# The context's norms: squares and the convolution's mean added up on GpSimd, one chunk summed on TensorE

## The chip, the cores and the metric

The kernel runs on one core of one Trainium2 chip. The metric is device time in microseconds of one execution, the median of several runs. All times below are microseconds (us) unless marked ns; the engines are TensorE (PE in the rows, PEld for its weight loads), VectorE (DVE), ScalarE (ACT), GpSimd (POOL) and SyncE (SP).

## What is computed

A first block works on 256 tokens of width 1024: an adaptive norm, two kinds of attention, and a mixture of 32 experts of which each token takes four. A second block of two layers follows, which has a second stream beside the tokens, 256 tokens of context (`ctx`). In its first layer the context goes through the whole layer; in the second it gives only keys and values. Cut to what matters here, the context's way through the first layer is:

```
hc  = modulate(rms_norm_2(xc, mix_pre_g), shc1, scc1)            # norm 1
pc  = hc @ w_in                                                  # q, k, v, gates, convolution input
y   = conv_general_dilated(gl, conv_w, ...) + conv_b             # 31 taps, each channel by itself
y   = silu(layer_norm(y, conv_norm_g, conv_norm_b))              # mean, then variance
yc  = (ga * a_out + gg * g_out + gc * c_out) @ w_out
xc  = xc + gc1 * rms_norm_2(yc, mix_post_g)                      # first residual
hc2 = modulate(rms_norm_2(xc, ffn_pre_g), shc2, scc2)            # the norm ahead of the FFN
xc  = xc + gc2 * rms_norm_2(sq_relu_mlp(hc2, w_ff1, w_ff2), ffn_post_g)   # last residual
```

`rms_norm_2(x, g)` is `x * rsqrt(mean(x * x) + 1e-6) * g` over the 1024 channels of a token; `layer_norm` takes the mean away first. There are five such sums of squares over the channels on the context's way (norm 1, the convolution's norm, first residual, the norm ahead of the FFN, last residual) and one plain mean (the convolution's). The context does not depend on the first block's tokens, so its layer can run at any time before the second block needs its keys and values.

## The kernel before

**Layout.** Channels lie on the 128 partitions, in `KC` = 8 chunks, and the 256 tokens `T` along the free axis: a tile of the stream is 128x8x256. A sum over the channels is therefore a sum over the chunks and over the partitions. TensorE does it: a chunk's 128 tokens are the stationary operand, a column of ones the moving one, and the result, one value for each of 128 tokens, adds up in PSUM over the chunks (`stats_add`, L194 to L203). One such sum over eight chunks and two halves of the tokens is 16 matmuls, and since an fp32 matmul leaves two records in the trace, 32 records of 128x1.

**A norm.** `norm_sums` (L245) takes the squares of two chunks at a time into a tile of 128x512, alternately on ScalarE (L252) and VectorE (L254), and sums each with `stats_add` (L200). `stats_end` (L216) computes the reciprocal root on VectorE with small operations of 128x2 (L163 to L173) and spreads it over the partitions with two transposes (`bcast_tok`, L179), on which the elementwise work of the norm waits. `folded_stats` (L261) is another form, which the last stage of the kernel uses: ScalarE squares the first four chunks in one operation, ScalarE and VectorE the next two pairs, GpSimd adds those onto the first four (L272) and halves the four chunks to two and to one (`fold`, L187, L192), and TensorE sums that one chunk. Where `self.side` is set, the tile of the squares is `sqs`, of which there is one buffer.

**Stages.** The first block runs in three stages, `front` (the attention), `route` (the choice of the experts) and `moe` (the 32 experts). The context's layer, `ctx_pass` (L1426), is laid between them as other work for the same engines: `prio` (L1760) calls `run_ctx` (L1786) after each step of a stage, as many times as the lists FRONT, ROUTE and MOE say (L1843 to L1845), and `run_ctx` sets `self.side` while it writes a piece of the context. A scheduler then orders the instructions of each engine when the program is built; at run time every engine takes its own in that order and waits where an operand is not there. The context's pieces have PSUM buffers of their own (`side`) and pools of their own (`cx`). `conv_norm` (L1617) is called by the context (L1539) and by the last stage (L1356). Two other callers of `norm_stats`, at L517 and L709, belong to the first block and run without `self.side`. The context's layer ends with a DMA of its result (L1575); the experts go on without it, and after them the two layers of the second block run on the tokens, with `self.tail` set.

**An expert.** The tokens of an expert stand in 32 or 64 columns (`hG`). Its gate and up weights (`raw`, L981) come by DMA, are the moving operand, and fill `mlin`; a bias is added by matmuls with `bgh` and `bgl` (L1036); VectorE and ScalarE compute the activation (`eg`, L920 to L925); TensorE transposes it (L987) and multiplies the down weights (L1006) into `main`; L897 and L898 put the result back to its tokens. The context's large products are L365 (`side`).

Of the kernel before, what the change touches and what calls it, by code (L numbers as in the profile page):

```python
# [15 lines left out]
OP = mybir.AluOpType  # L16
# [4 lines left out]
P = 128  # L21
D = 1024
KC = 8
GW = 128
T = 256
# [73 lines left out]
class Builder:  # L99
# [156 lines left out]
        return st  # L256

    def norm_stats(self, xT):
        return self.stats_end(self.norm_sums(xT), 1.0 / D)

    def folded_stats(self, xT, b):  # L261
# [1355 lines left out]
    def conv_norm(self, L, yc, chi, clo, pool):  # L1617
        nc = self.nc
        self.pop_conv(1000)
        if self.tail:  # L1620
            b = self.t(pool, [P, KC, T], tag="qn")[:, 0:4, :]
            nc.gpsimd.tensor_add(b, yc[:, 0:4, :], yc[:, 4:8, :])
            self.fold(b)
            mb = self.ps("tr")[:, :T]
            nc.tensor.matmul(mb, self.ones, b[:, 0, :], start=True, stop=True)
            for c in range(0, KC, 2):
                nc.vector.scalar_tensor_tensor(yc[:, c:c + 2, :], mb.unsqueeze(1).to_broadcast([P, 2, T]), -1.0 / D,
                                               yc[:, c:c + 2, :], op0=OP.mult, op1=OP.add)
            bc = self.folded_stats(yc, self.t(pool, [P, KC, T], tag="qn")[:, 0:4, :])
        else:  # L1630
            s = self.ps("tr")
            for c in range(KC):
                for t in range(2):
                    nc.tensor.matmul(s[:, t:t + 1], yc[:, c, t * P:(t + 1) * P], self.ones[:, 0:1],
                                     start=(c == 0 and t == 0), stop=(c == KC - 1), skip_group_check=True)
            mu = self.st([P, 2], tag="mu")
            nc.vector.tensor_scalar(mu, s[:, 0:2], 1.0 / D, None, op0=OP.mult)
            mb = self.bcast_tok([mu[:, 0:1], mu[:, 1:2]])
            for c in range(KC):
                nc.vector.tensor_sub(yc[:, c, :], yc[:, c, :], mb)  # L1640
            bc = self.norm_stats(yc)
        hb = self.st([P, KC], tag="hb")
        nc.vector.tensor_scalar(hb, L["cbn"], 0.5, None, op0=OP.mult)
        for k in range(KC):
            y = self.hk()
            nc.vector.scalar_tensor_tensor(y, yc[:, k, :], L["cg"][:, k:k + 1], bc, op0=OP.mult, op1=OP.mult)
            th = self.t(pool, [P, 512], tag="cth", bufs=2)[:, :T]
            nc.scalar.activation(th, y, AF.Tanh, scale=0.5, bias=hb[:, k:k + 1])
            nc.scalar.activation(y, y, AF.Identity, bias=L["cbn"][:, k:k + 1])
            nc.vector.scalar_tensor_tensor(y, th, 1.0, y, op0=OP.add, op1=OP.mult)  # L1650
            self.split(y, chi[:, k, :], clo[:, k, :], scale=0.5)
# [234 lines left out]
```

## Time and profile before

| | us |
| --- | --- |
| median of three runs | 2740.73 (2739.36 to 2746.4) |
| the profiled execution | 2745.34 |
| its span, first to last instruction | 2743.4 |
| TensorE busy in the span | 2590.6 (94%) |
| VectorE busy | 1605.5 (59%) |
| ScalarE busy | 1177.6 (43%) |
| GpSimd busy | 318.3 (12%) |

The mean granted clock of TensorE is 0.974 of full speed. In the trace the first block's attention and routing last up to about 300 us, the experts with the context's layer beside them to about 1275 us (the context's last DMA is at 1274.46), the experts alone to about 1520 us, and the two layers of the second block from about 1595 us to the end. Busy times of one engine can be read against the stretch they stand in; TensorE's records are pipelined, so that one begins before the last has ended.

### The profile page before, as it was taken

What the parts mean: (1) busy time and instruction counts of PE and PEld (TensorE: products, weight loads), DVE (VectorE), ACT (ScalarE), POOL (GpSimd) and SP (SyncE); (2) the same over time, 40 slices, a digit from 0 to 9 for tenths busy, and PEclk for the clock granted to TensorE, in tenths of its full rate; (3) what the DMA queues carried; (4) which work ended last, traced back from release to release, by engine and by line L of the source; (5) the groups of instructions that cost most, each with busy time, mean ns of one, the idle gap of its engine ahead of it and who ended that gap; (6) DMA issues with size and microseconds to landing.
All of it is one profiled execution on the core that took longest, in us unless ns stands there. A gap on an engine that the chain in (4) does not pass through costs nothing. (4 is left out here: it accounts for less than half of the span.)

```text
span 2743.4 us, 49770 instructions
## 1 busy us (share of the span) xinstructions
PE 2590.6 (94%) x20358; PEld 2046.6 (75%) x20359; DVE 1605.5 (59%) x3058; ACT 1177.6 (43%) x2019; POOL 318.3 (12%) x334
## 2 busy tenths in 40 slices
PE   7999999999899999999889879999999999999898
PEld 5656878678677767875333468888789998899898
DVE  3465543687654524433111269988556689897655
ACT  2343343333243323331111146785444566866544
POOL 0000000000000000000000015462001034461000
PEclk9989899999999999999999989999999999999999
DMA  9758599989999999999999935335764443335352
GB/s 400 300 222 296 199 384 418 371 342 403 387 360 385 394 377 355 409 419 367 397 383 421 422 147 185 124 105 219 259 223 174 184 179 132 140 135 185 146 193 85
DMA packets 119369, 769.79 MB, mean 281 GB/s; under 512 B 11632, under 2 KB 12016, under 8 KB 52832
## 3 DMA queue, kind: packets, MB, share of 16 engines
q1 hardware_dynamic: 117744, 759.15, 70.8%
q0 software_dynamic: 1392, 7.41, 0.7%
q8 instruction: 162, 2.65, 0.4%
q14 instruction: 71, 0.58, 0.1%
HBM read 762.84 MB, written 3.67 MB: 279 GB/s over the span
## 5 line engine op out<-in xcount | busy, mean ns | idle before, releaser
L343 DVE TENSOR_TENSOR wlo<-raw,whi 128x1024 fp32r<-128x1024 f32 (+1 forms) x288 | 338.5, 1178 | 163.0 <-ACT whi L342 155.6
L365 PE MATMUL lin<-hhi,wlo 128*128 128x256 f32 x1440 | 401.3, 284 | 10.0 <-DVE wlo L343 9.6
L365 PE MATMUL lin<-hhi,whi 128*128 128x256 f32 x1440 | 399.5, 281 | 3.7 <-ACT hhi L284 2.2
L365 PE MATMUL lin<-hlo,whi 128*128 128x256 f32 x1440 | 399.1, 279 | 0.1
L342 ACT ACTIVATE whi<-raw 128x1024 fp32r<-128x1024 f32 (+1 forms) x288 | 276.9, 964 | 236.0 <-PE lin L365 164.8
L981 PE MATMUL mlin<-raw,hG 128*32 128x256 f32 (+2 forms) x2920 | 344.0, 460 | 16.2 <-DMA raw<-in_w_gate_up_dram 16.2
L365 PEld LDWEIGHTS lin<-hhi,wlo 128*128 128x128 f32 x1440 | 269.4, 189 | 24.9 <-DVE wlo L343 19.1
L1590 POOL TENSOR_TENSOR yc<-yc,ctmp 128x256 f32<-128x256 f32 x240 | 247.4, 1049 | 301.1 <-ACT ctmp L1589 300.8
L343 DVE TENSOR_TENSOR wlos<-raws,whis 128x512 fp32r<-128x512 f32 x246 | 166.3, 688 | 194.2 <-ACT whis L342 184.1
L365 PEld LDWEIGHTS lin<-hhi,whi 128*128 128x128 f32 x1440 | 271.1, 189 | 9.2 <-ACT hhi L284 3.7
L365 PEld LDWEIGHTS lin<-hlo,whi 128*128 128x128 f32 x1440 | 272.5, 189 | 2.4 <-DVE hlo L285 1.2
L981 PEld LDWEIGHTS mlin<-raw,hG 128*32 128x32 f32 (+2 forms) x2920 | 130.9, 121 | 178.8 <-issue 114.6
L342 ACT ACTIVATE whis<-raws 128x512 fp32r<-128x512 f32 x246 | 149.1, 627 | 224.8 <-PE side L365 177.5
L365 PE MATMUL side<-hhi,whis 128*128 128x256 f32 x720 | 203.2, 288 | 0.0
L365 PE MATMUL side<-hlo,whis 128*128 128x256 f32 x720 | 199.7, 282 | 0.0
L365 PE MATMUL side<-hhi,wlos 128*128 128x256 f32 x720 | 193.1, 284 | 0.7 <-DVE wlos L343 0.5
L343 DVE TENSOR_TENSOR wlo<-raws,whi 128x1024 fp32r<-128x1024 f32 x108 | 139.6, 1293 | 77.3 <-ACT whi L342 74.5
L1592 DVE SCALAR_TENSOR_TENSOR yc<-gl,cw,yc 128x256 f32<-128x256 f32 x240 | 169.4, 736 | 1.5 <-ACT yc L1586 1.5
L342 ACT ACTIVATE whi<-raws 128x1024 fp32r<-128x1024 f32 x108 | 114.5, 1060 | 129.0 <-PE lin L365 89.0
L1006 PE MATMUL main<-raw,aT 128*32 128x256 f32 (+2 forms) x1408 | 160.9, 447 | 2.3 <-DMA raw<-in_w_down_dram 2.3
L365 PEld LDWEIGHTS side<-hhi,whis 128*128 128x128 f32 x720 | 136.7, 190 | 16.4 <-issue 12.0
L365 PE MATMUL lin<-ahi,wlo 128*128 128x256 f32 x528 | 144.0, 279 | 4.7 <-DVE wlo L343 4.6
(603 smaller groups left out, 5739.3 us busy)
## 6 DMA issues: line engine op xcount, KB each, us to landing
raw<-in_w_gate_up_dram SPq DMA_DIRECT2D x120, 2048.0 KB, 11.4
raw<-in_w_down_dram SPq DMA_DIRECT2D x55, 2048.0 KB, 11.0
raw<-in_w_in_dram SPq DMA_DIRECT2D x60, 1024.0 KB, 7.1
raws<-in_w_in_dram SPq DMA_DIRECT2D x95, 512.0 KB, 6.7
raws<-in_w_ff_dram SPq DMA_DIRECT2D x88, 512.0 KB, 8.3
raw<-in_w_ff_dram SPq DMA_DIRECT2D x44, 1024.0 KB, 7.1
phi<-in_ada_w_dram SPq DMA_DIRECT2D x10, 1024.0 KB, 7.3
plo<-in_ada_w_dram SPq DMA_DIRECT2D x10, 1024.0 KB, 7.0
```

The source lines that it names most:

```text
L342: x = nc.scalar.activation(flat(hi), flat(rows[i]), AF.Copy)
L343: y = nc.vector.tensor_sub(flat(lo), flat(rows[i]), flat(hi).bitcast(F32))
L365: x = nc.tensor.matmul(*args, skip_group_check=True, **kw)
L981: nc.tensor.matmul(d, hT(k), gu[k][c0 // D][:, c0 % D:c0 % D + W], start=False, stop=(k == KC - 1), skip_group_check=True)
L1006: nc.tensor.matmul(pys[h][g * C:(g + 1) * C, :W], st, dn[m][:, c0:c0 + W], start=(m == 0), stop=(m == KC - 1), skip_group_check=True)
L1590: nc.gpsimd.tensor_add(d, d, m)
L1592: self.paced(1, nc.vector.scalar_tensor_tensor(d, x, wcol, d, op0=OP.mult, op1=OP.add))
```

## The change

Two functions are changed, and both for the context alone.

```diff
     def norm_stats(self, xT):
+        if self.side:
+            return self.folded_stats(xT, self.t(self.cx, [P, 4, T], tag="kv"))
         return self.stats_end(self.norm_sums(xT), 1.0 / D)
...
     def conv_norm(self, L, yc, chi, clo, pool):
         nc = self.nc
         self.pop_conv(1000)
-        if self.tail:
-            b = self.t(pool, [P, KC, T], tag="qn")[:, 0:4, :]
...
-        else:
-            s = self.ps("tr")
-            for c in range(KC):
-                for t in range(2):
-                    nc.tensor.matmul(s[:, t:t + 1], yc[:, c, t * P:(t + 1) * P], self.ones[:, 0:1],
-                                     start=(c == 0 and t == 0), stop=(c == KC - 1), skip_group_check=True)
-            mu = self.st([P, 2], tag="mu")
-            nc.vector.tensor_scalar(mu, s[:, 0:2], 1.0 / D, None, op0=OP.mult)
-            mb = self.bcast_tok([mu[:, 0:1], mu[:, 1:2]])
-            for c in range(KC):
-                nc.vector.tensor_sub(yc[:, c, :], yc[:, c, :], mb)
-            bc = self.norm_stats(yc)
+        four = lambda: self.t(pool, [P, KC, T], tag="qn")[:, 0:4, :] if self.tail else self.t(pool, [P, 4, T], tag="kv")
+        b = four()
+        nc.gpsimd.tensor_add(b, yc[:, 0:4, :], yc[:, 4:8, :])
+        self.fold(b)
+        mb = self.ps("tr")[:, :T]
+        nc.tensor.matmul(mb, self.ones, b[:, 0, :], start=True, stop=True)
+        for c in range(0, KC, 2):
+            nc.vector.scalar_tensor_tensor(yc[:, c:c + 2, :], mb.unsqueeze(1).to_broadcast([P, 2, T]), -1.0 / D,
+                                           yc[:, c:c + 2, :], op0=OP.mult, op1=OP.add)
+        bc = self.folded_stats(yc, four())
         hb = self.st([P, KC], tag="hb")
```

The context's norms now go through `folded_stats`, with a tile of four chunks, `kv`, from the context's pool: one square over four chunks and one over two on ScalarE, one over two on VectorE, two adds and two folds on GpSimd, then two matmuls of 128x1 (four records) instead of 16. The convolution's mean is added up by GpSimd as well and summed and spread over the partitions by one matmul of 128x256, with the matrix of ones stationary and that chunk moving; the subtraction is four operations over two chunks on VectorE instead of eight over one. The last stage of the kernel did both in this form already. In the new kernel the line numbers are two higher from `norm_stats` to `conv_norm` and ten lower behind it.

On each engine the scheduler's order moves with it. TensorE has 16815 instructions instead of 16902, VectorE 3086 instead of 3096, GpSimd 378 instead of 355.

TensorE, from the end of the context's last product ahead of the first residual to the broadcast of the norm ahead of the FFN, before. `sqs` are tiles of squares, `rs_rs` the reciprocal root, `raw` an expert's weights, `main` the accumulator of its down product:

```order
L981 MATMUL mlin_9111<-raw_9104,hG_8599 32x256 x4
L200 MATMUL side_9385<-ones_72,sqs_9398 128x1 x4
L200 MATMUL side_9385<-ones_72,sqs_9404 128x1 x4
L179 MATMUL side_9422<-cst_68,rs_rs_9412 128x128 x2
...
L200 MATMUL side_9451<-ones_72,sqs_9458 128x1 x4
...
L987 MATMUL main_9191<-cst_68,eg_9184 128x128 x2
L200 MATMUL side_9451<-ones_72,sqs_9464 128x1 x4
L1006 MATMUL main_9200<-raw_9196,aT_8890 32x256 x16
L200 MATMUL side_9451<-ones_72,sqs_9470 128x1 x4
L1006 MATMUL main_9200<-raw_1688_9198,aT_8890 32x256 x16
L179 MATMUL side_9488<-cst_68,rs_rs_9478 128x128 x2
```

The same place in the new kernel:

```order
L983 MATMUL mlin_9067<-raw_9060,hG_8555 32x256 x4
L200 MATMUL side_9351<-ones_72,kv_9341 128x1 x2
L179 MATMUL side_9366<-cst_68,rs_rs_9356 128x128 x2
...
L200 MATMUL side_9405<-ones_72,kv_9395 128x1 x2
...
L989 MATMUL main_9147<-cst_68,eg_9140 128x128 x2
L179 MATMUL side_9420<-cst_68,rs_rs_9410 128x128 x2
...
L1008 MATMUL main_9156<-raw_9152,aT_8846 32x256 x16
```

Each norm has one row of sums instead of four, and the two groups of down matmuls that stood among the sums of the second norm now stand behind its broadcast.

TensorE at the last residual, before:

```order
L365 MATMUL side_13506<-phi_12797,wlos_13620 128x256
L200 MATMUL side_13675<-ones_72,sqs_13682 128x1 x2
L1006 MATMUL main_11790<-raw_2073_11788,aT_11354 32x256 x16
L200 MATMUL side_13675<-ones_72,sqs_13688 128x1 x4
L200 MATMUL side_13675<-ones_72,sqs_13694 128x1 x4
L897 MATMUL main_11831<-G_10211,yh_11827 128x256
...
L981 MATMUL mlin_12032<-raw_12024,hG_11542 64x512 x2
...
L179 MATMUL side_13712<-cst_68,rs_rs_13702 128x128 x2
```

and in the new kernel:

```order
L367 MATMUL side_13438<-phi_12729,wlos_13552 128x256
L989 MATMUL main_11711<-cst_68,eg_11704 128x128 x4
...
L1008 MATMUL main_11722<-raw_11718,aT_11286 32x256 x16
L200 MATMUL side_13617<-ones_72,kv_13607 128x1 x2
L179 MATMUL side_13632<-cst_68,rs_rs_13622 128x128 x2
L1008 MATMUL main_11722<-raw_2068_11720,aT_11286 32x256 x16
L983 MATMUL mlin_11964<-raw_11956,hG_11474 64x512 x2
```

The broadcast follows its sums directly; the second group of down matmuls, the next expert's gate and up matmuls and the combine rows, which stood ahead of it, stand behind it.

GpSimd around the first residual, before. `pick` prepares an expert's bias row, `m_` is the load of the context's own stream:

```order
L1020 CAST pick_9100<-sel_5192 128x288
L1020 CAST pick_9246<-sel_5192 128x288
L1553 DMA m_1704_9383<-in_ctxT_dram 128x2048
L1020 CAST pick_9532<-sel_5192 128x288
L1020 CAST pick_9863<-sel_5192 128x256
```

and in the new kernel:

```order
L1555 DMA m_1701_9339<-in_ctxT_dram 128x2048
L1022 CAST pick_9464<-sel_5180 128x288
L274 TENSOR_TENSOR kv_9341<-kv_9341,sqs_9343 128x512
L274 TENSOR_TENSOR kv_9341<-kv_9341,sqs_9346 128x512
L192 TENSOR_TENSOR kv_9341<-kv_9341 128x512
L192 TENSOR_TENSOR kv_9341<-kv_9341 128x256
L274 TENSOR_TENSOR kv_9395<-kv_9395,sqs_9397 128x512
L274 TENSOR_TENSOR kv_9395<-kv_9395,sqs_9400 128x512
L192 TENSOR_TENSOR kv_9395<-kv_9395 128x512
L192 TENSOR_TENSOR kv_9395<-kv_9395 128x256
L1022 CAST pick_9795<-sel_5180 128x256
```

The eight operations of the two norms stand between two experts' `pick` rows.

## Rows read from the trace of the kernel before

**Rows 1.** Busy time by stretch: stretch, length, PE, PEld, DVE, ACT, POOL, clock, DMA share, GB/s.

```profile
300.00:1275.00 975.00, 953.93 (x8465) 719.40 (x8465) 515.30 (x1130) 343.58 (x657) 13.40 (x29) 0.98 0.94 376
1275.00:1520.00 245.00, 214.66 (x1032) 87.14 (x1030) 44.34 (x88) 28.77 (x48) 2.81 (x7) 0.97 0.99 403
```

**Rows 2.** TensorE's waits from 300 to 1275 us, the largest: sum, count, longest.

```profile
PE mlin L981 <- DMA raw<-in_w_gate_up_dram: 6.5, 4, 4.3
```

**Rows 3.** Context's sums: L200's (ns least/mean/most), TensorE groups (busy, mean ns | idle before).

```profile
L200 PE MATMUL side<-ones,sqs x160: 164/250/373, 175.3 to 1259.1; 128*128 128x1 f32 x160
...
L200 PE MATMUL side<-ones,sqs 128*128 128x1 f32 x32 | 5.7, 298 | 1.6 <-DVE sqs L254 0.8 <-ACT sqs L252 0.8
...
L1634 PE MATMUL side<-ones,y 128*128 128x1 f32 x16 | 3.6, 353 | 0.4 <-DVE y L1592 0.4
```

**Rows 4.** TensorE at the convolution's norm: start, length, instruction.

```profile
726.28 0.77 PE L1036 MATMUL mlin<-bgh,pick 128*128 128x512 f32 x1
...
737.21 0.60 PE L200 MATMUL side<-ones,sqs 128*128 128x1 f32 x4
...
751.12 3.65 PE L981 MATMUL mlin<-raw,hG 128*64 128x512 f32 x16
```

**Rows 5.** The same view from the first residual to the norm ahead of the FFN.

```profile
887.26 1.93 PE L981 MATMUL mlin<-raw,hG 128*32 128x256 f32 x32
887.88 0.63 ACT L252 ACTIVATE sqs<-y 128x512 f32<-128x512 f32 x1
...
891.01 1.09 PE L200 MATMUL side<-ones,sqs 128*128 128x1 f32 x8 [0.84 <-DVE sqs L254]
...
894.02 0.66 PE L179 MATMUL side<-cst,rs_rs 128*128 128x128 f32 x2 [1.92 <-DVE rs_rs L173]
894.61 3.64 PE L981 MATMUL mlin<-raw,hG 128*32 128x256 f32 x32
...
901.41 0.42 DVE L1734 TENSOR_TENSOR m<-m,hks 128x256 f32<-128x256 f32 x1
...
912.04 0.43 PE L179 MATMUL side<-cst,rs_rs 128*128 128x128 f32 x2
```

**Rows 6.** GpSimd's groups in the whole span, all from the last stage: busy, mean ns | idle.

```profile
L192 POOL TENSOR_TENSOR qn<-qn 128x512 f32<-128x512 f32 x4 | 8.6, 2155 | 0.3
L212 POOL TENSOR_TENSOR sq<-sq,sq 128x512 f32<-128x512 f32 x4 | 6.4, 1612 | 363.5 <-ACT sq L1395 261.3 <-ACT sq L1369 102.1
L1622 POOL TENSOR_TENSOR qn<-yc 128x1024 f32<-128x1024 f32 x2 | 6.4, 3188 | 1.8 <-DVE yc L1592 1.8
L272 POOL TENSOR_TENSOR merged<-merged,sq 128x512 f32<-128x512 f32 x2 | 3.1, 1558 | 12.9 <-ACT sq L271 12.9
L192 POOL TENSOR_TENSOR sq<-sq 128x256 f32<-128x256 f32 x4 | 3.0, 738 | 0.3
```

**Rows 7.** Squares on VectorE: context's (ns least/mean/most); last stage's with GpSimd's add beside.

```profile
L254 DVE TENSOR_TENSOR sqs<-y x6: 683/691/693, 740.3 to 1257.5; 128x512 f32<-128x512 f32 x6
...
1880.88 2.33 POOL L272 TENSOR_TENSOR qn<-qn,sq 128x512 f32<-128x512 f32 x1 [11.53 <-ACT sq L271]
...
1881.98 1.78 DVE L269 TENSOR_TENSOR sq<-yc 128x512 f32<-128x512 f32 x1
```

**Rows 8.** TensorE at the last residual, and the busy times of one stretch there.

```profile
1254.53 1.93 PE L1006 MATMUL main<-raw,aT 128*32 128x256 f32 x32
...
1260.55 5.32 PE L981 MATMUL mlin<-raw,hG 128*64 128x512 f32 x16
...
1266.84 0.38 PE L179 MATMUL side<-cst,rs_rs 128*128 128x128 f32 x2
...
1264.00:1268.00 4.00, 4.00 (x24) 1.92 (x22) 1.30 (x4) 0.00 (x0) 0.00 (x0) 1.00 0.27 53
```

**Rows 9.** TensorE behind its longest wait; busy times of one stretch, the clock third last.

```profile
718.79 3.64 PE L981 MATMUL mlin<-raw,hG 128*32 128x256 f32 x32 [4.30 <-DMA raw<-in_w_gate_up_dram]
...
720.00:724.00 4.00, 3.59 (x30) 1.94 (x22) 4.00 (x12) 0.00 (x0) 0.00 (x0) 0.50 1.00 419
```

More of the change, by code (lines that the diff above doesn't have):

```diff
@@ L1619, in conv_norm @@
         self.pop_conv(1000)
-        if self.tail:
-            b = self.t(pool, [P, KC, T], tag="qn")[:, 0:4, :]
[L1622 to L1629, printed above, removed]
-        else:
-            s = self.ps("tr")
-            for c in range(KC):
-                for t in range(2):
-                    nc.tensor.matmul(s[:, t:t + 1], yc[:, c, t * P:(t + 1) * P], self.ones[:, 0:1],
-                                     start=(c == 0 and t == 0), stop=(c == KC - 1), skip_group_check=True)
-            mu = self.st([P, 2], tag="mu")
-            nc.vector.tensor_scalar(mu, s[:, 0:2], 1.0 / D, None, op0=OP.mult)
-            mb = self.bcast_tok([mu[:, 0:1], mu[:, 1:2]])
-            for c in range(KC):
-                nc.vector.tensor_sub(yc[:, c, :], yc[:, c, :], mb)
-            bc = self.norm_stats(yc)
+        four = lambda: self.t(pool, [P, KC, T], tag="qn")[:, 0:4, :] if self.tail else self.t(pool, [P, 4, T], tag="kv")
[8 more added lines that the diff above has]
+        bc = self.folded_stats(yc, four())
         hb = self.st([P, KC], tag="hb")
```

## The prediction

> **What bounds the kernel now.** I read the busy times by stage first, then TensorE's waits, then what the replaced work costs, then its places in the order of time. The change works between the start and 1275 us. From 300 to 1275 us TensorE is busy for 953.93 of 975 us, with the DMA engines busy 0.94 of the time; VectorE works 515.30 us there and GpSimd 13.40 [rows 1]. The stage after it, MoE alone, is the transfers': DMA share 0.99, TensorE 214.66 of 245 us. So up to 1275 us TensorE's queue sets the pace as long as weights arrive, with little room in the transfers, and GpSimd is free. What TensorE waits for is short: its largest item is 6.5 us in all, for gate and up weights [rows 2]. A saved TensorE microsecond can therefore count, but so does any wait that a longer chain of GpSimd makes.
>
> **What the change removes.** Each of five context norms now sums 8 chunks by 32 matmul records of 128x1; the group is 160 records [rows 3]. Eight of them take 1.09 us [rows 5], so 160 take 160/8 x 1.09 = 21.8 us (by the front's 32 in 5.7 us [rows 3], up to 28). The convolution's mean is 16 records more, 3.6 us, with 0.4 of waiting for the last taps [rows 3]. I count another 2.2 us, an estimate: that its end at 1.2 GHz holds back the rows behind it, which begin at 726.28 [rows 4]; the two transposes of the mean are 0.6 more (such a pair takes 0.66 [rows 5]). What comes back to TensorE is 5 times four records at 0.5 us and one 128x256 matmul at 0.3 to 0.6. Net 21.8 + 3.6 + 2.2 + 0.6 - 2.5 - 0.6 = 25 us of TensorE work less. If nothing else moved, that would be the gain, 0.9%.
>
> **What it adds: a chain.** Before, the sums of early chunks ran on TensorE while the later squares were still being made, and MoE matmuls stood between them. Now one row must wait for a chain: a square on ScalarE of two chunks (0.63 us [rows 5]), a GpSimd add of 128x512, VectorE's square of the last two chunks (0.69 [rows 7]; it writes the one buffer of that name, so it waits for that add), a second add, a fold at 128x512, one at 128x256. No such GpSimd work stands in this stage before, so I bound it by the tail's: an add takes 1.56 us at the least (`merged` [rows 6]) and 2.33 beside VectorE's work [rows 7]; a fold of 512 takes 2.16 and at the least 1.61, as an add of that size does; one of 256 0.74, or by half of the 2.16 1.08 [rows 6]. VectorE's square takes 1.78 us where GpSimd's add lies beside it [rows 7]. Low end 0.63 + 1.56 + 0.69 + 1.56 + 1.61 + 0.74 = 6.8 us; high end 0.63 + 2.33 + 1.78 + 2.33 + 2.16 + 1.08 = 10.3. I take 7.8, the low end and 1 us for six hand-overs, since VectorE does little besides at these places.
>
> The Trainium skill, GPSIMD Engine Reference, sections 3.1 and 4.1, speaks against the change: an elementwise add of two inputs belongs on VectorE, where it takes about half GpSimd's time. Its figure, 4497 ns for 2048 elements, would make some 1.1 us of a 512-element add and as little of a fold, as an estimate, which the trace does not bear out: it has 1.56 to 2.33. By the page's figure the chain would be some 1.6 us shorter at four places, the sum below -3 instead of +3.3, and the time 2738.
>
> **Place by place.** TensorE takes its rows in order, so I compare how long the same rows take from one fixed point to the norm's broadcast (L179), and correct for MoE work that the new order has moved behind it.
>
> *Norm 1, in the front stage.* The 32 records there took 5.7 us with 1.6 us of waiting [rows 3]. The new chain is as long, and the front's own chain goes on through other engines: -3 us, bounds -6 and 0.
>
> *Convolution.* The mean's 3.6 + 2.2 + 0.6 = 6.4 us go. Its three GpSimd steps (3.19 + 2.16 + 1.08 = 6.4 us [rows 6]) have cover: the rows from 726.28 to 737.21, 10.9 us [rows 4], stand ahead of the new mean matmul. Without that cover they cost 6.4. From 737.21 to the broadcast, which follows the row that ends at 754.77, it was 17.5 us. Now: mean matmul 0.6, two subtractions on VectorE 1.4 (at the square's 0.69 [rows 7]), a square over four chunks 1.1 (an estimate, twice the 0.63 less its start), chain 7.8, sums 0.5, and the gate and up rows that stand ahead of the broadcast as before, 3.65 (the row at 751.12 [rows 4]): 15.0. Another 3.65 us of gate and up rows have moved behind it, so 18.6 for the same work. 18.6 - 17.5 - 6.4 = -5.3, bounds -6.3 and -2.8 by the chain's ends.
>
> *First residual.* TensorE is free for its sums at 889.2 us (887.26 + 1.93 [rows 5]). The first square begins at 887.88, so the chain ends at 895.7: TensorE stands still for 6.5 us (bounds 5.5 to 9) with its MoE rows behind that one row. Then 0.5 for the sums and 1.92 for the rsqrt: broadcast at 898.1 instead of 894.02, +4.1. From that go the sixteen records of the first four chunks, which TensorE ran before 887.26, 2 x 1.09 = 2.2 us: +1.9, bounds +0.9 and +4.4.
>
> *The norm ahead of the context's FFN.* Broadcast to broadcast it was 912.04 - 894.02 = 18.0. The last chunks are ready 7.8 us in (901.41 and 0.42 [rows 5]), the first six earlier, so ScalarE's second square comes at about 5.5. Then 5.5 + 7.8 + 0.5 + 1.92 = 15.7, and two groups of 16 down matmuls have moved behind it, 2 x 1.93 = 3.9: 19.6, so +1.6, bounds +0.6 and +4.1. VectorE's square that waits for the first add has the swiglu of the next expert queued behind it, and ScalarE and TensorE wait for that; this is the wait that the change adds on VectorE, and it lies inside the 7.8.
>
> *Last residual.* From the row at 1254.53 to the broadcast at 1266.84 it was 12.3 us, filled with one group of down rows, one of gate and up (5.32), and combine rows, of which a group fills what lies between 1265.87 and the broadcast, 1.0 [rows 8]. Now the row of sums stands behind an earlier group of down rows, so the chain begins 1.93 sooner; it is 0.6 + 7.8 + 0.5 + 1.92 = 10.8 long, and behind the broadcast 1.93 of down, 3.65 of gate and up (the undisturbed group's) and two such groups of combine rows are still to do: -1.9 + 10.8 + 7.6 = 16.5, +4.2; the two earlier pairs of records, 1.1 us, go: +3.1, bounds +2.1 and +5.6. In 1264 to 1268 us the DMA share is 0.27 [rows 8]: the transfers wait for TensorE just there, so this passes on into the transfer-bound stage.
>
> The chip's clock comes on top. After the 4.30 us wait at 718 us the gate and up group takes 3.64 us instead of 1.93, and the granted clock is 0.50 in 720 to 724 us, which is 1.2 of its 2.4 GHz [rows 9]; after the 0.84 and 1.92 us waits at the first residual the same group takes 3.64 as well, and 1.93 some microseconds before [rows 5]. Some of the old idle already costs this; the new waits make such stretches at the convolution, the FFN norm and the last residual, at 3.64 - 1.93 = 1.7 us for each group at the low clock, and some three groups' worth after a long wait. I take +5, bounds +2 and +14.
>
> Sum: -3 - 5.3 + 1.9 + 1.6 + 3.1 + 5 = +3.3; bounds -6.7 and +25 if all are low or all high together. So the waits hand back what TensorE saves. GpSimd's library load, which the order of the new kernel has near the start, is hidden, since GpSimd has nothing urgent there, and the tail's rows keep their order. The profiled execution's own time, 2745.34 us, would become 2748.6; it lies 4.6 us above the median of the runs shown, and from that median, 2740.73, I get 2744.
>
> **The rivals.** *Slower:* GpSimd beside VectorE at the dear end, chain 10.3 us, and TensorE at 1.2 GHz for long stretches after each wait. It decides from a chain of about 9 us on, where the wait is longer than the 4.30 us one that had the large price. Convolution -2.8, residual +4.4, FFN norm +4.1, last +5.6, front -3, clock +8: +16.3, so 2757. For it: TensorE has nothing else in its queue once the row waits. Against: VectorE does little at these places.
>
> *Faster:* the waits fall into time in which the next weights would not have been there, so they cost nothing, and the low chain holds: front -6, convolution -6.3, the middle norms and the last +0.5 in all, clock +1: -10.8, so 2730. For it: DMA share 0.94, and 6.5 us of TensorE's waits are for weights. Against: they are four waits in 975 us [rows 2], and 0.27 right at the last place.
>
> *Nothing:* the transfers set the length up to 1520 us, and both savings and waits vanish in them: 2741, within 3. For it: 0.94 and 0.99 [rows 1]. Against: TensorE is busy for 953.93 of the same 975 us.
>
> **How the numbers follow.** Forecast 0.42, slower 0.28, faster 0.12, nothing 0.18. A measurement of this kernel tells 0.3%, 8.2 us, from no change. The forecast stays within that in five of six cases, with most of the rest above; the slower case lies above it and the faster one below, each but for a small part; nothing lies within. That makes faster 0.12, same 0.55, slower 0.33. The range takes in the forecast with its clock's high end, the slower case, and about half of the faster one: 2731 to 2760.
>
> **What would show it.** In the changed kernel: GpSimd adds of 1.6 to 2.3 us in the context's norms; TensorE rows of L200 that wait 5 to 9 us for GpSimd at the first residual and the last; a stretch at granted clock 0.50 behind each; the mean's matmul at the convolution without a wait; TensorE some 25 us less busy up to 1275 us but the context's end no earlier than 1274. A chain under 6 us, or an end before 1265, would make it wrong on the fast side; a wait of over 10 us at one place, or MoE's weights arriving later after it, on the slow side.

## The result and the profile after

The changed kernel takes 2763.28 us (median of six runs, 2752.67 to 2767.9) beside 2746.43 for the kernel before in the same measurement (2739.36 to 2749.44): a ratio of 1.006, 95% interval 1.0044 to 1.0076. It is slower by some 17 us. A second measurement of it (e4, below) gives 2758.97 and 1.0052 (1.0033 to 1.0072). The prediction had 2744 and a range of 2731 to 2760.

The trace of after is of the execution that took 2752.67, the fastest of its six, with a span of 2750.9 us. Busy time by stretch, with the columns of [rows 1]:

```profile
300.00:1275.00 975.00, 930.91 (x8255) 697.70 (x8254) 510.18 (x1111) 347.99 (x655) 37.25 (x48) 0.97 0.93 372
1275.00:1520.00 245.00, 216.48 (x1068) 87.37 (x1068) 48.44 (x97) 29.50 (x49) 2.79 (x7) 1.00 1.00 414
```

TensorE works 23 us less from 300 to 1275 us, and 24.5 us less counted from the start, as the sum said; GpSimd works 24 us more. The DMA engines moved 372 GB/s there instead of 376. TensorE's waits from 300 to 1275 us, with the columns of [rows 2]:

```profile
PE side L200 <- POOL kv L192: 17.8, 4, 5.9
PE mlin L1038 <- DVE eg L922: 5.4, 2, 5.2
PE mlin L983 <- DMA raw<-in_w_gate_up_dram: 4.0, 3, 3.1
PE side L179 <- DVE rs_rs L173: 3.8, 2, 1.9
```

The four waits for GpSimd, 17.8 us, are new and take most of what TensorE saves. The 5.2 us wait for an expert's activation (`eg`) stands at the convolution. The chain at the first residual, and what TensorE then does, in order of time:

```profile
886.05 0.63 ACT L273 ACTIVATE sqs<-y 128x512 f32<-128x512 f32 x1
886.76 1.26 POOL L274 TENSOR_TENSOR kv<-kv,sqs 128x512 f32<-128x512 f32 x1 [22.09 <-ACT sqs L273]
888.06 0.69 DVE L271 TENSOR_TENSOR sqs<-y 128x512 f32<-128x512 f32 x1 [2.65 <-POOL kv L274]
888.83 1.64 POOL L274 TENSOR_TENSOR kv<-kv,sqs 128x512 f32<-128x512 f32 x1 [0.81 <-DVE sqs L271]
890.55 2.06 POOL L192 TENSOR_TENSOR kv<-kv 128x512 f32<-128x512 f32 x2
892.67 1.01 PE L200 MATMUL side<-ones,kv 128*128 128x1 f32 x4 [5.31 <-POOL kv L192]
895.60 0.66 PE L179 MATMUL side<-cst,rs_rs 128*128 128x128 f32 x2 [1.92 <-DVE rs_rs L173]
...
907.64 1.01 PE L200 MATMUL side<-ones,kv 128*128 128x1 f32 x4 [5.90 <-POOL kv L192]
...
913.26 3.64 PE L1008 MATMUL main<-raw,aT 128*32 128x256 f32 x32
...
923.06 1.93 PE L1008 MATMUL main<-raw,aT 128*32 128x256 f32 x32
```

The steps are those foreseen: VectorE's square begins as soon as the first add has read the buffer, and TensorE takes its row 0.1 us behind the last fold. From the first square to that row it is 6.6 us. The two last lines matter most: the down matmuls of an expert, which in the kernel before stood between these sums:

```profile
905.74 3.50 PE L1006 MATMUL main<-raw,aT 128*32 128x256 f32 x32
...
910.14 1.93 PE L1006 MATMUL main<-raw,aT 128*32 128x256 f32 x32
```

They come 7.5 and 12.9 us later. They read the buffers (`raw`) that the next expert's weights need, so SyncE's queue, which issues the loads, waits for them. Its waits for down matmuls from 895 to 925 us, among waits for other rows, first before and then after (L947 and L949 are the load of the gate and up weights):

```profile
SPq L947 <- PE main L1006: 7.3, 1, 7.3
...
SPq L949 <- PE main L1008: 14.5, 1, 14.5
```

and the stretch from 900 to 920 us in the same two traces, with the DMA share next to last:

```profile
900.00:920.00 20.00, 18.57 (x216) 12.91 (x208) 11.70 (x34) 6.42 (x15) 0.40 (x1) 0.91 0.96 388
...
900.00:920.00 20.00, 12.99 (x107) 9.10 (x100) 11.76 (x35) 5.57 (x12) 5.42 (x5) 0.74 0.63 237
```

With a queue that waits 14.5 us before its next load, the DMA engines stand partly idle: 0.63 busy instead of 0.96. To follow this through a whole trace I add up (1 - DMA share) x 20 us over the 64 stretches of 20 us from 280 to 1560 us. This **idle sum** is 70.4 us before and 76.4 after. It stands beside the **end of the experts** (the load of `kall` on GpSimd, among the first rows of the last two layers), 1595.3 and 1597.9 us.

### The profile page after: what moved, and what is told of

Its sections match the earlier page's. It is cut to its first block, busy times and chain, and to the rows that moved or that the text cites. A ratio compares the mean times of both kernels' runs of the same rounds, so it can differ in the third digit from the quotient of the medians.

```text
span 2750.9 us, 49422 instructions
## 1 busy us (share of the span) xinstructions
PE 2573.2 (94%) x20186; PEld 2025.9 (74%) x20187; DVE 1607.6 (58%) x3048; ACT 1183.7 (43%) x2019; POOL 346.1 (13%) x357
```

## The experiments

The first table row is the kernel before, whose trace is that of the front part; e8 is another execution of it. "Ratio" is to the kernel before in the same measurement, with its 95% interval. Idle sum, end of the context (its last DMA) and end of the experts come from each kernel's one trace, so they need not be those of its median run.

| kernel | median us (runs) | ratio | idle sum | context ends | experts end |
| --- | --- | --- | --- | --- | --- |
| before | 2746.43 (6) | 1 | 70.4 | 1274.5 | 1595.3 |
| before, e8 | 2741.94 (1) | | 68.0 | 1274.4 | 1590.9 |
| after | 2763.28 (6) | 1.006 (1.0044 to 1.0076) | 76.4 | 1273.4 | 1597.9 |
| after, e4 | 2758.97 (6) | 1.0052 (1.0033 to 1.0072) | 74.6 | 1270.7 | 1600.9 |
| e1 mean only | 2757.61 (10) | 1.0042 (1.002 to 1.0064) | 82.0 | 1276.8 | 1604.1 |
| e2 norms only | 2754.46 (10) | 1.0034 (1.0012 to 1.0057) | 69.6 | 1266.9 | 1590.6 |
| e3 no adds | 2749.15 (10) | 1.0016 (0.9999 to 1.0033) | 63.0 | 1221.5 | 1585.5 |
| e5 VectorE adds | 2740.67 (10) | 0.9988 (0.9975 to 1.0001) | 63.4 | 1250.7 | 1590.7 |
| e12 the same | 2742.23 (10) | 0.9979 (0.9961 to 0.9997) | 60.0 | 1244.6 | 1583.3 |
| e6 two norms plain | 2758.23 (4) | 1.0055 (1.0035 to 1.0076) | 77.4 | 1272.2 | 1606.0 |
| e7 sums ordered late | 2780.18 (4) | 1.0119 (1.0102 to 1.0136) | 98.8 | 1452.1 | 1627.3 |
| e9 norm 1 on VectorE | 2756.0 (10) | 1.0037 (1.0021 to 1.0052) | 69.8 | 1261.0 | 1594.3 |
| e10 late norms on VectorE | 2754.27 (10) | 1.0031 (1.0018 to 1.0044) | 76.8 | 1272.9 | 1609.6 |
| e11 norm 1 plain | 2745.61 (10) | 1.0002 (0.9985 to 1.002) | 69.2 | 1255.2 | 1593.5 |

Over these 14 traces the end of the experts follows the idle sum (correlation 0.96, and 0.91 without e7), 1.1 us for each us that the transfers stand idle; the end of the context goes with it less closely (0.85, and 0.70 without e7). That is a relation between traces and not yet a cause, and after's 6.0 us of idle time more than before are well under its 14 to 17 us.

### One part of the change at a time (e1, e2)

```diff
 e1, against after
     def norm_stats(self, xT):
-        if self.side:
-            return self.folded_stats(xT, self.t(self.cx, [P, 4, T], tag="kv"))
...
-        bc = self.folded_stats(yc, four())
+        bc = self.folded_stats(yc, four()) if self.tail else self.norm_stats(yc)
 e2, against before
     def norm_stats(self, xT):
+        if self.side:
+            return self.folded_stats(xT, self.t(self.cx, [P, 4, T], tag="kv"))
```

> The kernel before with the convolution's mean alone added up on GpSimd; the five norms sum eight chunks on TensorE as before. Theory A (the waits of TensorE behind GpSimd's chains at the two residuals and the FFN norm cost the time): the mean has its cover, so this is not slower than before, about 2741 to 2746, and perhaps 3 to 6 faster. Theory B (the loss begins at the convolution, where the transfers' share falls from 0.96 to 0.92 in 700 to 800 us): about half of the loss is here, 2752 to 2757.

> The kernel before with the five context norms folded on GpSimd; the convolution's mean is TensorE's as before. Theory A: nearly the whole loss is here, 2758 to 2766. Theory B: about half of it, 2752 to 2757.

Both cost more than half of the whole, 0.42% and 0.34%, so the parts do not add up. Theory A falls with e1: there GpSimd's adds have their cover, and TensorE waits for none of them, yet it is 12 us slower. Its stretch from 900 to 920 us, 170 us behind the edit, at norms that e1 does not touch, shows where part of that may go:

```profile
900.00:920.00 20.00, 17.07 (x120) 11.66 (x116) 9.78 (x30) 4.16 (x9) 0.40 (x1) 0.59 0.66 242
```

The DMA share is 0.66, as in after. What e1 changes there is only the scheduler's order, which it works out anew behind an edit: the second group of down matmuls stands behind the norm's broadcast, at 917.89 us. The mean alone also gives nothing where it stands, which is shown below with the steps of the prediction.

### TensorE's saving without the chain (e3)

```diff
 against after
-            nc.gpsimd.tensor_add(b[:, 2 * j:2 * j + 2, :], b[:, 2 * j:2 * j + 2, :], sq)
-        self.fold(b)
+            if not self.side:
+                nc.gpsimd.tensor_add(b[:, 2 * j:2 * j + 2, :], b[:, 2 * j:2 * j + 2, :], sq)
+        if not self.side:
+            self.fold(b)
...
+        b = yc
+        if self.tail:
+            b = four()
```

> The changed kernel without GpSimd's adds and folds in the context: TensorE sums the first chunk as soon as ScalarE has squared it, and the mean is that of one chunk; this leaves most of the sums out, so it has the whole saving of TensorE without the chain. If TensorE sets the pace up to 1275 us, it gives the saving of some 25 us: about 2720. If the transfers set it, the saving vanishes: 2738 to 2746. If the new places of the experts' rows cost the time and not the waiting, it stays slow, 2755 or more.

With most of the saving (21.7 us up to 1275 us) and no chain it is not faster: 1.0016. Its context ends 53 us earlier than before, and its experts 10 (5 beside the other trace of before, e8):

```profile
1221.48 0.54 POOL L1579 DMA_DIRECT2D cd<-m  x1 [5.07 <-DVE m L1728]
1585.47 0.73 POOL L1819 DMA_DIRECT2D kall<-kcd  x1 [0.33 <-issue]
```

So a context that is done earlier leaves the experts alone earlier, in the stretch where the transfers are at 0.99 [rows 1], and most of the gain is lost there. Why the 5 to 10 us do not appear in the median either is not shown; the last section has what e3's trace says of it.

### A second trace of each (e4, e8)

> The changed kernel again, for a trace of an execution nearer to its median of 2763.28 than the one at 2752.67. Theory A: the experts stand some 16 us late after the FFN norm and keep 8 to 16 of them to the end of the experts, about 1530. Rival: the experts' end is again only 3 us late, and the rest is in the two last layers, which the change does not touch.

> The kernel before again, for a second trace: how far its stages vary from one execution to another. Theory C expects the DMA engines' idle time to the end of the experts to be again some 70 us, and the rest of the scatter to lie in the two last layers; the rival, that the traces compared so far differ by chance, expects 75 to 80.

e4 has the experts 10 to 14 us late from the norm ahead of the FFN to the end of the context and 5.6 us late at their end; the rest of its span, 2762.9, lies in the last two layers: 1162.0 us in e4, 1153.1 in after, 1148.2 and 1149.0 in the two traces of before. So one trace each does not give the 14 to 17 us of the medians; it shows places, and the medians decide.

### The same chain on VectorE (e5, e12)

```diff
 against after, in fold, folded_stats and conv_norm
-            nc.gpsimd.tensor_add(b[:, 2 * j:2 * j + 2, :], b[:, 2 * j:2 * j + 2, :], sq)
+            (nc.vector if self.side else nc.gpsimd).tensor_add(b[:, 2 * j:2 * j + 2, :], b[:, 2 * j:2 * j + 2, :], sq)
```

> The changed kernel with the context's adds and folds on VectorE instead of GpSimd, in the norms and in the convolution's mean. Theory C (TensorE stands still behind the chain; its down products are late, the weight buffers come free late, the DMA engines stand idle and that is never made up): a chain shorter by 2 to 3 us at each place gives back about half of the loss, 2750 to 2756. Rival D (the new places of the experts' rows cost the time, whichever engine adds): as slow as the changed kernel, 2759 to 2763.

> The kernel of e5_vec_adds again, beside the others on the same chip, since its 2740.67 was below the kernel before by less than the interval: 2738 to 2744 if the gain of 0.1 to 0.2% is there, 2745 and more if it was chance.

This gives back all of the loss, more than theory C expected, and makes the fastest of the kernels that compute the whole result. Against the kernel before it is at 0.9988 and 0.9979; that is less than the 0.3% that the text ahead named, though e12's interval ends below 1. The adds in it, VectorE's group (least, median, most, in ns), and TensorE's waits from 300 to 1275 us:

```profile
L274 DVE TENSOR_TENSOR kv<-kv,sqs x10: 672/692/693, 175.9 to 1236.5; 128x512 f32<-128x512 f32 x10
...
PE mlin L983 <- DMA raw<-in_w_gate_up_dram: 10.2, 5, 4.3
PE side L200 <- DVE kv L192: 5.5, 3, 4.1
```

The waits for the chain fall from 17.8 to 5.5 us and those for weights rise from 4.0 to 10.2: TensorE, with less to do, now waits for the transfers.

### Which of the two: the chain or the order (e6, e7, e9, e10, e11)

e5 has another order of TensorE's rows than after, not only a shorter chain. Five kernels are to take these apart.

```diff
 e6, against after: the first residual and the norm ahead of the FFN on TensorE
-        if self.side:
+        if self.side and not self.plain:
 e7, against after: a norm's sums behind the last down matmul written
+        if n0 is not None:
+            self.behind(self.firstmm, n0)
 e9 and e10, against after
+    def adder(self):
+        return self.nc.vector if self.side and self.place in ON_VEC else self.nc.gpsimd
+ON_VEC = (1,)          # e9: norm 1
+ON_VEC = (3, 4, 5)     # e10: the residuals and the norm ahead of the FFN
 e11, against after: norm 1 on TensorE
-        if self.side:
+        if self.side and not self.first:
```

> The changed kernel with the first residual and the norm ahead of the FFN summed on TensorE as before; norm 1, the convolution's norm and mean and the last residual stay on GpSimd. The experts' rows stand at these two places as in the changed kernel. Theory C: the DMA idle time at 900 to 920 us (share 0.63 in the changed kernel, 0.96 before) goes back by some 5 us, 2752 to 2756. Rival D: it stays, 2758 or more.

> The changed kernel, in which the sums of each context norm are ordered on TensorE behind the last down product written before them, so that GpSimd's chain runs beside the experts' rows. Theory C: TensorE's 18 us of waiting for GpSimd fall below 8 and the time to about 2745 to 2750. Rival E (TensorE's order is of no account, GpSimd's own work slows the others): it stays at 2759 or more. If the context is late by this order and ends after the experts have begun to use its buffers, it is slower than the changed kernel.

> The changed kernel with one edit: in norm 1 alone, in the front stage, VectorE adds and folds instead of GpSimd. The other four norms and the mean keep GpSimd's chains. With this TensorE's order from the experts on is that of e5_vec_adds but for four rows. Theory D (the order of the experts' rows, which the scheduler works out anew from the first norm on, sets the time): as e5_vec_adds, 2738 to 2746. Theory C (the waits for GpSimd's chains at the later places set it): little better than the changed kernel, 2754 to 2760.

> The changed kernel with VectorE's adds and folds at the first residual, the norm ahead of the FFN and the last residual; norm 1 and the convolution keep GpSimd's. TensorE's order is that of the changed kernel but for 20 rows at the last residual. Theory C: the chains are 2 to 3 us shorter at three places, so 2746 to 2752. Theory D: the order is that of the changed kernel and so is the time, 2756 to 2762.

> The changed kernel with norm 1 summed on TensorE as before, the other four norms and the mean on GpSimd. At the norms TensorE has as many of the experts' matmuls behind it as in e5_vec_adds. Theory D: 2738 to 2746. Theory C: 2754 to 2760.

e9 against e5 was meant as the pair for the chain: TensorE's order is the same but for four rows, and the chains of the convolution and the last three norms run on GpSimd in one and on VectorE in the other. 2756.0 against 2740.67 and 2742.23 makes 14 us. e9's waits for them:

```profile
PE side L204 <- POOL kv L196: 10.5, 4, 3.6
```

But e11 has these four chains on GpSimd too, with 10.0 us of waits for them, norm 1 on TensorE, and nearly e9's order, and it is at 2745.61: 3 to 5 us above e5 and e12. By its expectation e11 speaks for theory D and e9 for theory C. The two traces hardly differ from the experts on (idle sums 69.2 and 69.8, experts' ends 1593.5 and 1594.3), but ahead of them they do. In e9, TensorE's granted clock from 200 to 220 us is 0.51, about its lower level of 1.2 GHz, and the experts' first `pick` comes 6.9 us later than in e11; e9 first, then e11:

```profile
200.00:220.00 20.00, 17.48 (x74) 7.03 (x66) 12.81 (x64) 7.87 (x29) 0.00 (x0) 0.51 0.71 261
308.83 1.16 POOL L1026 CAST pick<-sel 128x288 fp32r<-128x288 f32 x2 [9.52 <-DVE ov L806]
...
200.00:220.00 20.00, 17.21 (x119) 9.25 (x119) 15.73 (x80) 11.20 (x41) 0.00 (x0) 1.00 0.95 366
301.91 1.16 POOL L1025 CAST pick<-sel 128x288 fp32r<-128x288 f32 x2 [10.57 <-DVE ov L805]
```

In e5 and e12 it comes at 305.43 and 304.30 us, so e9's trace starts its experts later than theirs too, ahead of every chain in which they differ. Over all executions e9's mean granted clock is 0.971 and e11's 0.974. e9's trace is of its fastest execution but one, so whether this makes the 10 us between e9 and e11 stays open, and the 14 us can't be put down to the chain.

e10, in the order of after, with VectorE at three of the places, stays at 2754.27, where theory D wanted 2756 and more and theory C 2752 at most; that is 5 to 9 us better than after and 12 to 14 worse than e5, whose order it lacks, along with VectorE's adds at two places. The stage ahead of its experts has the low clock as well (0.53 from 200 to 220 us, first `pick` at 308.83).

e6 has the order of after at the two middle norms, and TensorE's sums as before. The share at 900 to 920 us comes back from 0.63 to 0.88, but not the time: 2758.23 is theory D's. Its idle sum, 2.8 us below that of after at 960 us, is above it from 1440 us on. Without a chain its two groups of down matmuls come about as late as those of after (913.26 and 923.06):

```profile
913.27 1.93 PE L1009 MATMUL main<-raw,aT 128*32 128x256 f32 x32
...
921.46 1.93 PE L1009 MATMUL main<-raw,aT 128*32 128x256 f32 x32
```

Three experts' activations (`et`) stand around the two norms. The start of the first and of the last of them, in before, after, e6, e5 and e9:

```profile
L923 ACT ACTIVATE et<-eg x3: 417/418/420, 853.4 to 933.1; 128x256 f32<-128x256 f32 x3
...
L925 ACT ACTIVATE et<-eg x3: 417/418/418, 859.1 to 952.3; 128x256 f32<-128x256 f32 x3
...
L926 ACT ACTIVATE et<-eg x3: 416/417/418, 859.1 to 950.7; 128x256 f32<-128x256 f32 x3
...
L925 ACT ACTIVATE et<-eg x3: 402/419/419, 865.3 to 938.4; 128x256 f32<-128x256 f32 x3
...
L929 ACT ACTIVATE et<-eg x3: 401/419/419, 866.9 to 942.6; 128x256 f32<-128x256 f32 x3
```

It is 79.7 us before, 93.2 in after and 91.6 in e6, where TensorE sums, but 73.1 in e5 and 75.7 in e9, where GpSimd's chain stands. So at this place the order costs some 12 us (e6 against before) and the chain 1.6 to 2.6 (after against e6, e9 against e5). What of this reaches the end differs (experts' ends in the table), and how the whole 14 to 17 us divide is not shown: by e11 the order has the larger part, by e9 the chain.

e7 went wrong as its last sentence feared, and more: the sums waited for rows of later experts, the context ended at 1452 us, and 35 us were lost, with only 6.1 us of waits for GpSimd. Waits taken from TensorE by delaying the context are not a gain.

### Fewer transfers (e13, e14, e15)

```diff
 against before, e5 and after
-        dn = []
+        dn = [self.xw[:, j % 2, :] for j in range(4)] if solo != "only" else []
```

> The kernel before with half of each expert's down weights left unloaded: four of the eight chunks of that product take a tile that is in SBUF anyway, so TensorE does the same work and the transfers of an expert fall by a sixth. Base for the next two. If the transfers set the pace of the experts, it is 60 to 110 us faster than the kernel before; if TensorE does, less than 40.

> The same cut in e5_vec_adds, which has TensorE's whole saving of some 25 us and the short chain. With fewer transfers TensorE sets the pace, so the saving that was worth 3 to 5 us beside the full transfers should show: 12 to 25 us faster than e13. Rival (the saving is lost for another reason than the transfers): within 5 us of e13.

> The same cut in the changed kernel. Where TensorE sets the pace, the prediction's sum holds: some 25 us saved against 18 us of waits and 5 of the clock, so -5 to +5 of e13, and 10 to 20 slower than e14. Rival (what the chains cost is only the transfers they hold up): as fast as e14.

Measured: e13 2729.64 (0.9951, 0.9934 to 0.9968), e14 2731.63 (0.9951, 0.9935 to 0.9968), e15 2718.21 (0.9901, 0.9875 to 0.9927). A sixth of the experts' transfers gone gives 15 us, not the 60 to 110 of transfers that set the pace; e13 falls under its other case, that TensorE does. TensorE is a limit close by: it is busy for 1500 of the 1573 us to the end of e13's experts. With the transfers eased, the changed kernel is 11 us faster than its base, with intervals that do not touch, where its expectation had it within 5: TensorE's saving, lost beside the full transfers, may be worth something there. But e14, with the same saving and the shorter chain, gains nothing over e13, as its rival had it. In e14's trace the granted clock from 200 to 220 us is 0.61 and the first `pick` comes at 312.81 us, against 301.24 in e13 and 305.10 in e15; whether that is the reason is open, as with e9. The three also have orders of their own. So "the transfers set the end" is too simple. Two limits stand close together, and the experiments do not part the order, the chain and the clock beside them.

## Why the prediction was wrong, step by step

- **TensorE's work: right.** 25 us less predicted, 24.5 measured up to 1275 us.
- **The context's end: right**, 1273.4 us, "no earlier than 1274" but for half a microsecond.
- **Norm 1: not shown.** -3 us foreseen; the first expert's activation came 3.0 us earlier, at 349.11 instead of 352.09 us. But the second trace of before (e8, the last row) has it at 347.93, so two executions of one kernel differ by more.

```profile
352.09 0.42 ACT L923 ACTIVATE et<-eg 128x256 f32<-128x256 f32 x1 [1.84 <-DVE eg L920]
...
349.11 0.42 ACT L925 ACTIVATE et<-eg 128x256 f32<-128x256 f32 x1 [1.17 <-DVE eg L922]
...
347.93 0.42 ACT L923 ACTIVATE et<-eg 128x256 f32<-128x256 f32 x1 [1.02 <-DVE eg L920]
```

- **The convolution's mean: the term was wrong.** It stood at -6.4 us. Much of the time of the 16 records of [rows 3] was one in which TensorE would have waited anyway: they begin at 722.85 us, and VectorE begins the activation that the next rows need at 723.90. With them gone, TensorE waits 5.19 us for that activation, which stands on VectorE behind the last taps of the convolution:

```profile
721.37 0.77 PE L1038 MATMUL mlin<-bgh,pick 128*128 128x512 f32 x1 [5.19 <-DVE eg L922]
...
734.38 0.70 PE L1627 MATMUL side<-kv,ones 128*128 128x256 f32 x2
...
743.68 1.01 PE L200 MATMUL side<-ones,kv 128*128 128x1 f32 x4 [3.15 <-POOL kv L192]
```

  The prediction took busy records for work on the path without asking what the next row was waiting for. From the first gate and up row of this place to the norm's broadcast it is 35.9 us before (718.79 to 754.70) and 38.0 after (712.82 to 750.80), with one gate and up group fewer in it, where the sum had -5.3. The cover that it named for the three GpSimd steps was there: the new mean matmul (L1627) stands without a wait.
- **The chain: shorter than thought.** 7.8 us predicted at the first residual, 6.6 measured. GpSimd's add takes 1.26 us where no VectorE row lies beside it and 1.64 where one does (at 888.83), so the 1.56 of the last stage was no low end. The Trainium skill, GPSIMD Engine Reference, section 3.1, from which the estimate was 1.1 us, was nearer than the rows, and its section 4.1, that such adds belong on VectorE at about half the time, is what e5 shows: 0.69 us an add there. With the adds there the loss is gone, though e5 has another order as well. The prediction set that page aside for rows of another stage.
- **The waits: near at the first residual, not at each place.** 5.31 us at the first residual where 6.5 had been foreseen; 5.90 at the norm ahead of the FFN; at the last residual 3.46, where 5 to 9 had been named; and 3.15 at the convolution, where none had been named.
- **The clock: about right in size, and not parted from the rest.** +5 us foreseen. Added up as the idle sum is, (1 - granted clock) x 20 us from 300 to 1280 us is 24.0 and 24.2 us in the two traces of before and 30.8 and 25.8 in the two of after: 2 to 7 us more. Over whole executions the clock's mean is 0.975 to 0.976 before and 0.970 to 0.972 in after and e4 (medians), and the slower executions of a kernel tend to be those with the lower clock. How far it is a cause, and how far it only follows from the waits, no run shows.
- **What the moved rows cost: the step that failed.** At the middle norms the sum charged each group of experts' down matmuls behind the broadcast at its own length, 1.93 us, and so took the new order as nearly free. But those groups came 7.5 and 12.9 us late, and they hold the weight buffers: SyncE's queue waited 14.5 us for one of them and the DMA engines fell to 0.63. The lateness is the order's and not the wait's: in e6, with no chain at these norms, the groups are 7.5 and 11.3 us late and the time is 2758.23, and e1, whose norms are TensorE's, loses 12 us. The share at 900 to 920 us is 0.88 in e6 and 0.66 in e1, without a chain, and 0.99 in e9's order with GpSimd's chain. The text had a clue, "this passes on into the transfer-bound stage", and used it for the last residual alone. How much of the whole loss is this, and how much the chains elsewhere and the clock, stays open.
- **What a saving is worth.** The 25 us were set off at full price against the waits. e3, which has most of the saving and no chain, is not faster than before. The rival "nothing" had that half and left out what the change could still cost.
- **The rival "slower"** had the side and nearly the size, 2757, but not the mechanism: its point of decision was a chain of 9 us, and the chain was 6.6. That it came near is luck.

## What to carry to other kernels

Where one stage is close to two limits, price a row that moves by what it holds: here down matmuls held weight buffers, and where they came late the transfers stood idle. Before counting a removed instruction as a gain, look at what the next row on its engine waits for. And where a scheduler sets the order, an edit in an early place moves rows hundreds of microseconds further on, so test the edit's parts each by itself, and don't expect them to add up.

## What was not expected of the hardware

TensorE's pace differs between executions at the same granted clock. In 2600 to 2700 us, where it runs products of one kind without a break, clock 1.00 in both, the trace of before and that of e3 have:

```profile
2600.00:2700.00 100.00, 100.00 (x885) 100.00 (x884) 60.78 (x62) 50.39 (x59) 0.00 (x0) 1.00 0.54 199
...
2600.00:2700.00 100.00, 100.00 (x851) 100.00 (x850) 58.54 (x61) 49.01 (x58) 0.00 (x0) 1.00 0.51 183
```

885 records against 851. From start to start of two such matmuls it is 113.3 ns there in before, after and eleven other traces, and 117.7 to 117.8 in those of e3, e13, e14 and e15. Over the 1780 or so such intervals of e3's last 250 us that is about 8 us, over half of what its last two layers took longer (1162.1 instead of 1148.2), and these longer layers hide the earlier end of the experts in that trace; whether e3's other executions ran so is not known. The last two layers of e4 took 1162.0 us at 113.3 ns there, so this is not the only scatter. It may be one reason why runs of this kernel scatter by some 10 us, and it is one why a single trace can't settle a difference of 0.5%.
